# A three-group encoder layer in split fp32: another order of the last down products, and norms on VectorE

## The chip, the cores and the metric

The kernel runs on one core of one Trainium2 chip. The metric is the device time of one execution in microseconds; of the kernel before, three executions were timed, and one more was run under the hardware profiler.

## The reference

One layer of an encoder with post-norm and residual factor `ALPHA`, for a prompt of 512 tokens and a sample of 1024 tokens, width 1024, feed-forward width 4096, all in fp32:

```python
x = layer_norm(x, ln_in_g, ln_in_b)
x = layer_norm(ALPHA * x + token_mixer(x, w_in, rpb, g_mix_a, g_mix_b, w_out), ln1_g, ln1_b)
x = layer_norm(ALPHA * x + memory_cross_attention(x, mem, w_xq, w_xkv, w_xo), ln2_g, ln2_b)
x = layer_norm(ALPHA * x + squared_relu_mlp(x, w_up, w_down), ln3_g, ln3_b)
...
def squared_relu_mlp(x, w_up, w_down):
    return jnp.square(jax.nn.relu(x @ w_up)) @ w_down
```

`token_mixer` is dilated and neighbourhood attention, each half of its result under an rms norm, times `w_out`. `memory_cross_attention` has 4 heads over 256 memory tokens.

## The kernel before

The tokens form three groups of 512: group 0 is the prompt, 1 and 2 are the sample; a group has four tiles of 128 tokens. PE multiplies fp32r numbers, so each fp32 operand is split into a high part (a copy on ACT) and a low part (a subtraction on DVE or POOL), and each product is three matmuls: high x high, high x low, low x high.

The program runs in stages: memory keys and values, the mixers, the output projections (`y_tile`, `w_out_half` for groups 0 and 1, `w_out_part` for group 2), `ln1`, then `heads(gi, extra)` for the cross-attention of each group, then the MLP of group 0 (32 blocks up and down), and the MLP of the sample by seven products of a Strassen-like scheme, first UP, then DOWN. The order of instructions on each engine is set by the scheduler of the tile framework, which goes by the program's order, priorities and its own timing; tiles come from pools with a fixed number of buffers (tags such as tok 8, qt, pt, gb, kv 2 each, q 7, cpr 2, wh and wl 3, wraw 2), and a new tile waits for an old one's last reader.

`heads` takes a table `extra`: under the key (head, half) stand functions that are called in the midst of that head, so that one group's projections and norms lie beside another group's attention. In `heads(1, ...)` (L887 on) the four parts of group 2's output projection and its four norms `ln1(2, t)` are placed so. A `w_out_part` is accumulated into the tok tiles by DVE (L725). `layer_norm` (L148) takes its statistics on DVE (L154 to L157), raises the variance to -1/2 on POOL (`pow`, L158), subtracts the mean and multiplies by g on DVE (L162); then, with `spread=1`, ACT scales by 1/sigma (L169) and POOL adds b (L173); with `spread=0` a second DVE operation (L164) does both; with `spread=2` the first half takes L164's form at L167 and the second half has ACT scale and DVE add (L171). `split_t` transposes the normed tile on PE (L137), copies the high part out (L139) and subtracts for the low part on DVE (L140); the results are x10, x11, x12 by group, and y1 for the projections' input.

A DOWN product i has a left side of hidden blocks (one, or a sum or difference of two), a right side of blocks of `w_down`, and goes with a sign into one or two of four output blocks `accs`. It has 16 chunks; a chunk is 4 token tiles x 3 matmuls into 4 PSUM banks. `left_parts` (L1079) makes the left sum on DVE in a wraw tile (L1085), copies the high part on ACT (L1088) and subtracts on DVE (L1089). `right` loads a block to a q tile and a second one added onto it by a DMA of POOL's queue (L993), or subtracts two on DVE (L1003), and splits with L1008 (ACT) and L1009 (DVE). `collect` (L1099) empties a bank into `accs` on DVE (L1103, L1105). The last product, number 2, does the first three banks over 16 chunks and keeps the split right sides in `kept` tiles; meanwhile group 0 of the sample is finished (`finish`, a `layer_norm` with the statistics of L1072); then bank 4 takes 48 matmuls, for which the left side is made a second time, 128 columns at a time; then comes group 1's last tile.

```python
UP, DOWN = (5, 3, 2, 4, 1, 7, 6), (3, 5, 4, 7, 1, 6, 2)
1: (((0, 0), SUB, (1, 1)), ((0, 0), SUB, (1, 1)), (((0, 0), ADD), ((1, 1), ADD))),
2: (((1, 0), SUB, (1, 1)), ((0, 0),), (((1, 0), ADD), ((1, 1), SUB))),
6: (((1, 0), SUB, (0, 0)), ((0, 0), ADD, (0, 1)), (((1, 1), ADD),)),
```

## Time and profile before

| what | value |
|---|---|
| runs | 2379.4, 2380.44, 2386.65 us; median 2380.44 |
| profiled execution | 2383.99 us, of which 2382.2 is the span of its instructions |
| mean granted clock of PE | 0.990 |
| DOWN, from its first matmul to its last | 2042.88 to 2372.67 |
| heads(1), the part with group 2's projection and norms | about 1155 to 1248 |
| first norms ln1(0) | about 880 to 905 |

A row of the profile names the line, the engine, the operation and the tiles written and read. A wait is idle time of an engine just before an instruction, put down to what released it. The granted clock is a share of full speed (2.4 GHz); 0.5 is the lower of two levels (1.2 GHz), and a value in between is a mean over both.

### The profile page before, as it was taken

Reading aid. Unit: us, or ns where it says so; the run is one execution under the profiler, and the core shown is the slowest. Engines: PE = TensorE matmul, PEld = TensorE weight load, DVE = VectorE, ACT = ScalarE, POOL = GpSimd, SP = SyncE. Lnnn points to the kernel's source line nnn. Section 1 sums busy time; section 2 is a strip of 40 time slices with the busy share of each in tenths; the row PEclk is TensorE's granted clock in tenths of the full one; section 3 lists DMA queues with packets and bytes.
Section 4 is the critical chain, followed back from the end, with each engine's and each line's share of the span. In section 5 each row is a group of like instructions: output and inputs, shape, how many; then the busy total and the mean of one; then the engine's idle time right before and its main releaser. Section 6 shows DMA issues by size and latency. Waiting matters only on the chain. (4 is left out here: it accounts for less than half of the span.)

```text
span 2382.2 us, 33165 instructions
## 1 busy us (share of the span) xinstructions
PE 2293.0 (96%) x11128; PEld 1903.7 (80%) x11128; DVE 1614.3 (68%) x3305; ACT 1044.8 (44%) x2216; POOL 930.9 (39%) x836
## 2 busy tenths in 40 slices
PE   7999999999999999999989999999999999999987
PEld 6877788899888777878867877788888888888865
DVE  5256545777657776558566586777766686686987
ACT  4346655666555534333333333333354222344443
POOL 7555443222334125433154355555541324213152
PEclk9999999999999999999999999999999999999998
DMA  9676345544445543435325454444589999859762
GB/s 322 197 195 183 91 108 135 123 109 112 108 114 130 170 133 106 142 110 182 107 89 177 124 159 142 141 134 136 162 231 200 204 250 232 208 139 196 196 163 71
DMA packets 401530, 371.02 MB, mean 156 GB/s; under 512 B 72000, under 2 KB 317776, under 8 KB 401360
## 3 DMA queue, kind: packets, MB, share of 16 engines
q1 hardware_dynamic: 358352, 335.34, 47.8%
q0 software_dynamic: 43008, 33.56, 10.0%
q8 instruction: 88, 1.44, 0.3%
q14 instruction: 82, 0.67, 0.1%
HBM read 290.76 MB, written 52.98 MB: 144 GB/s over the span
## 5 line engine op out<-in xcount | busy, mean ns | idle before, releaser
L107 POOL TENSOR_TENSOR wl<-wraw,wh 128x512 fp32r<-128x512 f32 x80 | 106.0, 1340 | 173.9 <-ACT wh L106 158.5
L465 ACT ACTIVATE q<-q,st 128x256 f32<-128x256 f32 (+3 forms) x256 | 138.6, 546 | 70.7 <-DVE st L464 64.7
L1008 ACT ACTIVATE wh<-q 128x512 fp32r<-128x512 f32 x176 | 110.0, 626 | 134.6 <-DMA q<-in_w_up_dram 73.0
L1009 DVE TENSOR_TENSOR wh<-q,wh 128x512 fp32r<-128x512 f32 x176 | 126.1, 718 | 54.8 <-ACT wh L1008 54.5
L993 POOL DMA_DIRECT2D q<-in_w_up_dram x64 | 82.9, 1470 | 182.1 <-DVE h L1046 73.6
L312 POOL TENSOR_TENSOR wl<-wraw,wh 128x256 fp32r<-128x256 f32 x128 | 94.7, 763 | 143.3 <-ACT wh L311 122.2
L511 DVE TENSOR_TENSOR pt<-t,pt 128x512 fp32r<-128x512 f32 x160 | 105.4, 671 | 60.0 <-ACT pt L510 59.0
L946 POOL TENSOR_TENSOR wl<-pt,wh 128x512 fp32r<-128x512 f32 x64 | 91.5, 1450 | 118.9 <-ACT wh L945 118.8
L993 POOL DMA_DIRECT2D q<-in_w_down_dram x64 | 56.4, 976 | 199.5 <-DVE wraw L1085 66.1
L510 ACT ACTIVATE pt<-t 128x512 fp32r<-128x512 f32 x160 | 89.4, 583 | 75.3 <-PE o L523 72.4
L107 POOL TENSOR_TENSOR wl<-qt,wh 128x512 fp32r<-128x512 f32 x64 | 101.7, 1609 | 50.8 <-ACT wh L106 42.8
L523 PE MATMUL o<-pt,tok 128*128 128x256 f32 (+3 forms) x560 | 111.1, 312 | 4.0 <-ACT q L529 2.6
L119 POOL TENSOR_TENSOR wl<-wraw,wh 128x512 fp32r<-128x512 f32 x48 | 62.3, 1311 | 134.3 <-ACT wh L118 134.3
L959 DVE TENSOR_TENSOR tok<-tok,t 128x512 f32<-128x512 f32 x124 | 82.9, 680 | 37.0 <-PE t L131 37.0
L959 DVE TENSOR_TENSOR tok<-tok,s 128x512 f32<-128x512 f32 x124 | 83.9, 680 | 29.6 <-PE s L131 29.4
L131 PE MATMUL pj<-x20h,wl 128*128 128x512 f32 x256 | 101.2, 395 | 2.7 <-POOL wl L107 2.4
L129 PE MATMUL pj<-x20h,wh 128*128 128x512 f32 x256 | 100.6, 393 | 0.3 <-ACT wh L106 0.2
L130 PE MATMUL pj<-x20l,wh 128*128 128x512 f32 x256 | 100.0, 391 | 0.0
L507 PE MATMUL t<-ident,q 128*128 128x128 f32 x624 | 95.2, 273 | 5.0 <-ACT q L465 3.6
L1088 ACT ACTIVATE wh<-wraw 128x512 fp32r<-128x512 f32 (+2 forms) x96 | 53.0, 557 | 106.9 <-issue 42.3
L106 ACT ACTIVATE wh<-wraw 128x512 fp32r<-128x512 f32 x80 | 47.7, 626 | 103.5 <-PE pj L131 24.8
L945 ACT ACTIVATE wh<-pt 128x512 fp32r<-128x512 f32 x64 | 36.9, 624 | 122.0 <-PE s L131 103.0
(494 smaller groups left out, 7677.4 us busy)
## 6 DMA issues: line engine op xcount, KB each, us to landing
q<-in_w_up_dram SPq DMA_DIRECT2D x128, 256.0 KB
q<-in_w_down_dram SPq DMA_DIRECT2D x128, 256.0 KB
wraw<-in_w_in_dram SPq DMA_DIRECT2D x96, 256.0 KB
qt<-in_w_up_dram SPq DMA_DIRECT2D x32, 512.0 KB
pt<-in_w_down_dram SPq DMA_DIRECT2D x32, 512.0 KB
q<-in_w_up_dram POOLq DMA_DIRECT2D x64, 256.0 KB, 8.1
q<-in_w_down_dram POOLq DMA_DIRECT2D x64, 256.0 KB, 6.2
sa<-kv SPq DMA_DIRECT2D x28, 512.0 KB
```

The costliest lines, as they stand in the source:

```text
L107: G.tensor_sub(wl[:, sl], r, f32(wh[:, sl]))
L129: T.matmul(out, lh[k], rh[k], start=(k == 0), stop=False, skip_group_check=True)
L130: T.matmul(out, lh[k], rl[k], start=False, stop=False, skip_group_check=True)
L131: T.matmul(out, ll[k], rh[k], start=False, stop=(k == n - 1), skip_group_check=True)
L465: A.activation(p, p, AF.Exp, bias=nm, scale=scale, accum_out=den)
L507: T.transpose(t[:, x:x + P], p, ident)
L511: V.tensor_sub(lo[:, 0:x], t[:, 0:x], f32(hi[:, 0:x]))
L523: T.matmul(o[:, q0:q0 + n], v(c, h), part[:, x:x + n], start=(done == 0 and part is hi), stop=(done == total - 1 and part is lo), skip_gro ...
L959: V.tensor_add(x, x, q)
L993: G.dma_start(out, src, accum_op=ADD)
L1008: A.activation(dst[0], x, AF.Copy)
L1009: low.tensor_sub(dst[1], x, f32(dst[0]))
```

## The change

- `ln1` calls `layer_norm` with `spread=0`, for all three groups.
- `heads(1)`: two of group 2's `w_out_part` calls stand at (1, 1) and the last at (2, 0); the norms stand at (2, 1) and (3, 0). The tile Y[2] is made ahead of `heads(0)`.
- DOWN's order is 4, 7, 1, 5, 3, 6, 2. The squares of block (1, 1) are taken in UP's last product, those of (0, 0) in DOWN's first.
- The left sums of products 2 and 6 are made in place, in the hidden blocks (1, 1) and (0, 0), by `left_sum` (L1081 after the change).
- Group 0 of the sample is finished in product 6 with `spread=0`; g3 lies in cpr tiles and b3 in q tiles, loaded after product 3.
- In the last product the left high parts of all chunks stay in tok tiles and the low parts of the last 128 columns in a qt and a pt tile, so that bank 4 uses parts made before. The four tiles of group 1 are collected and finished after it.

Lines behind L884 have other numbers after the change: L1009 is L1010, L1003 is L1004, L1085 is L1081, L1089 is L1093 (and L1095 for 128 columns), L1105 is L1111, L1072 is L1073.

```diff
--- before.py
+++ after.py
@@ -726,7 +726,7 @@
 
     def y_tile(gi, t):
         r, row = req(gi), 0 if gi < 2 else 512
-        if t == 0:
+        if gi not in Y:
             Y[gi] = new_act(f"y{gi}")
         rows = slice(row + t * P, row + (t + 1) * P)
         if toks[gi][t] is None:
@@ -774,7 +774,7 @@
         if t == 0:
             X1[gi] = new_act(f"x1{gi}")
             GB[gi] = [[bcast(d[n][0], "gb")] for n in ("ln1_g", "ln1_b")]
-        layer_norm(toks[gi][t], *GB[gi], 1)
+        layer_norm(toks[gi][t], *GB[gi])
         split_t(toks[gi][t], *X1[gi], t * P)
 
     def qt(gi, h, c):
@@ -881,11 +881,12 @@
         ln1(0, i)
         if i < 2:
             w_out_half(1, i)
+    Y[2] = new_act("y2")
     heads(0, {(h, 0): [call(ln1, 1, h)] for h in range(4)} | {(h, 1): [call(y_tile, 2, h)] for h in range(4)})
     heads(1, {(0, 0): [call(ln2, 0, 0), call(ln2, 0, 1)], (0, 1): [call(ln2, 0, 2), call(ln2, 0, 3)],
-              (1, 0): [call(w_out_part, 2, 0)], (1, 1): [call(w_out_part, 2, 1)],
-              (2, 0): [call(w_out_part, 2, 2)], (2, 1): [call(w_out_part, 2, 3)],
-              (3, 0): [call(ln1, 2, 0), call(ln1, 2, 1)], (3, 1): [call(ln1, 2, 2), call(ln1, 2, 3)]})
+              (1, 0): [call(w_out_part, 2, 0)], (1, 1): [call(w_out_part, 2, 1), call(w_out_part, 2, 2)],
+              (2, 0): [call(w_out_part, 2, 3)], (2, 1): [call(ln1, 2, 0), call(ln1, 2, 1)],
+              (3, 0): [call(ln1, 2, 2), call(ln1, 2, 3)]})
     heads(2, {(h, 0): [call(ln2, 1, h)] for h in range(4)})
     w_xo_part(2, 3)
     for t in range(4):
@@ -905,7 +906,7 @@
         6: (((1, 0), SUB, (0, 0)), ((0, 0), ADD, (0, 1)), (((1, 1), ADD),)),
         7: (((0, 1), SUB, (1, 1)), ((1, 0), ADD, (1, 1)), (((0, 0), ADD),)),
     }
-    UP, DOWN = (5, 3, 2, 4, 1, 7, 6), (3, 5, 4, 7, 1, 6, 2)
+    UP, DOWN = (5, 3, 2, 4, 1, 7, 6), (4, 7, 1, 5, 3, 6, 2)
 
 
     def left(i, k):
@@ -1044,7 +1045,7 @@
                     A.activation(h, o, AF.Copy, scale=1.0 if op == ADD else -1.0)
                 else:
                     V.tensor_tensor(h, h, o, op=op)
-            b = {2: (0, 1), 7: (1, 0), 6: (0, 0)}.get(i)
+            b = {2: (0, 1), 7: (1, 0), 6: (1, 1)}.get(i)
             if b is not None:
                 square(b, f)
 
@@ -1076,18 +1077,23 @@
         row = 512 * h + t * P
         S.dma_start(outs[1][0, row:row + P], accs[h][t])
 
-    def left_parts(lw, c, t0, t1):
-
-        n = (t1 - t0) * P
-        x = hidden(lw[0], c)[:, t0 * P:t1 * P]
-        if len(lw) > 1:
-            y = wp.tile([P, 512], F32, name="wraw", tag="wraw", bufs=2)[:, 0:n]
-            V.tensor_tensor(y, x, hidden(lw[2], c)[:, t0 * P:t1 * P], op=lw[1])
-            x = y
+    def left_sum(lw, c, y):
+        V.tensor_tensor(y, hidden(lw[0], c), hidden(lw[2], c), op=lw[1])
+
+    def left_parts(lw, c, summed=None, hi=None, last=None):
+
+        x = hidden(summed or lw[0], c)
+        if len(lw) > 1 and summed is None:
+            x = wp.tile([P, 512], F32, name="wraw", tag="wraw", bufs=2)
+            left_sum(lw, c, x)
         a = wp.tile([P, 1024], F32R, name="wh", tag="wh")
-        A.activation(a[:, 0:n], x, AF.Copy)
-        V.tensor_sub(a[:, 512:512 + n], x, f32(a[:, 0:n]))
-        return [(a[:, j * P:(j + 1) * P], a[:, 512 + j * P:512 + (j + 1) * P]) for j in range(t1 - t0)]
+        hi, lo = a[:, 0:512] if hi is None else hi, a[:, 512:1024]
+        n = 512 if last is None else 384
+        A.activation(hi, x, AF.Copy)
+        V.tensor_sub(lo[:, 0:n], x[:, 0:n], f32(hi[:, 0:n]))
+        if last is not None:
+            V.tensor_sub(last, x[:, n:512], f32(hi[:, n:512]))
+        return [(hi[:, j * P:(j + 1) * P], last if j * P == n else lo[:, j * P:(j + 1) * P]) for j in range(4)]
 
     def chunk(banks, ls, rs, c):
         for o, (lh, ll) in zip(banks, ls):
@@ -1104,43 +1110,53 @@
             else:
                 V.tensor_tensor(x, x, o, op=op)
 
+
+    inplace = {2: (1, 1), 6: (0, 0)}
+    g3 = b3 = None
     for n, i in enumerate(DOWN[:-1]):
         lw, rw, into = PRODUCTS[i]
         banks = [bank(tag) for tag in (("pj", "pj", "s", "s") if n % 2 == 0 else ("t", "t", "t", "o"))]
         for c in range(16):
-            ls = left_parts(lw, c, 0, 4)
+            ls = left_parts(lw, c, inplace.get(i))
             chunk(banks, ls, right(rw, down_block(c), V, "wl"), c)
             if n == 0:
-                square((1, 1), c)
+                square((0, 0), c)
+            if i == (5, 3)[c % 2]:
+                left_sum(PRODUCTS[2][0], c, hidden(inplace[2], c))
+            if i == 3:
+                left_sum(PRODUCTS[6][0], c, hidden(inplace[6], c))
+            if i == 6 and c % 4 == 2:
+                finish(0, c // 4, 0)
         for t in range(4):
             collect(into, t, banks[t])
-        if i in (5, 1):
+        if i in (5, 3):
             for t in range(4):
-                stats(0, t, 1 if i == 5 else 0)
+                stats(0, t, int(i == 3))
+        if i == 3:
+            g3, b3 = [slot("cpr") for _ in range(2)], [slot("q", 512) for _ in range(2)]
+            for q, name in ((g3, "ln3_g"), (b3, "ln3_b")):
+                for j in range(2):
+                    src = d[name][0]
+                    S.dma_start(q[j], bass.AP(tensor=src.tensor, offset=src.offset + 512 * j, ap=[[0, P], [1, 512]]))
 
 
     lw, rw, into = PRODUCTS[DOWN[-1]]
-    g3, b3 = ([slot("q", 512) for _ in range(2)] for _ in range(2))
-    for q, name in ((g3, "ln3_g"), (b3, "ln3_b")):
-        for j in range(2):
-            src = d[name][0]
-            S.dma_start(q[j], bass.AP(tensor=src.tensor, offset=src.offset + 512 * j, ap=[[0, P], [1, 512]]))
-    kept = []
+    kept, ls, rs = [], [], []
     banks = [bank(tag) for tag in ("pj", "pj", "s", "s")]
     for c in range(16):
         if c % 8 == 0:
             kept.append([act.tile([P, 8, 512], F32R, name="kept", tag="act") for _ in range(2)])
-        rs = right(rw, down_block(c), V, dst=[k[:, c % 8] for k in kept[c // 8]])
-        chunk(banks[0:3], left_parts(lw, c, 0, 3), rs, c)
-        if c % 4 == 3:
-            finish(0, c // 4, 1)
-    for t in range(3):
+            kept_lo = slot("qt" if c == 0 else "pt", dt=F32R)
+        if c % 2 == 0:
+            kept_hi = slot("tok", dt=F32R)
+        rs.append(right(rw, down_block(c), V, dst=[k[:, c % 8] for k in kept[c // 8]]))
+        ls.append(left_parts(lw, c, (1, 1), kept_hi[:, c % 2 * 512:c % 2 * 512 + 512],
+                             kept_lo[:, c % 8 * P:c % 8 * P + P]))
+        chunk(banks[0:3], ls[c][0:3], rs[c], c)
+    for c in range(16):
+        chunk(banks[3:4], ls[c][3:4], rs[c], c)
+    for t in range(4):
         collect(into, t, banks[t])
-    for c in range(16):
-        chunk(banks[3:4], left_parts(lw, c, 3, 4), [k[:, c % 8] for k in kept[c // 8]], c)
-    for t in range(4):
-        if t == 3:
-            collect(into, 3, banks[3])
         finish(1, t, 2 if t == 3 else 1)
```

The scheduler moves instructions at places that the diff does not tell. On DVE in heads(1), from the first norm of group 2 on, the order before was (tok holds the projection, lnst the statistics, gb gains and offsets, cpr the attention's probabilities):

```order
L162 SCALAR_TENSOR_TENSOR tok<-tok,lnst,gb 128x1024
L725 TENSOR_TENSOR tok<-tok,o 128x512
L810 RECIPROCAL cst<-cst 128x2
L156 BN_AGGR lnst<-lnst 128x2
L725 TENSOR_TENSOR tok<-tok,pj 128x512
L812 TENSOR_SCALAR cpr<-cpr,cst 128x256 x2
L157 TENSOR_SCALAR lnst<-lnst 128x1
L162 SCALAR_TENSOR_TENSOR tok<-tok,lnst,gb 128x1024
L725 TENSOR_TENSOR tok<-tok,pj 128x512
```

and is now:

```order
L162 SCALAR_TENSOR_TENSOR tok<-tok,lnst,gb 128x1024
L725 TENSOR_TENSOR tok<-tok,o 128x512
L156 BN_AGGR lnst<-lnst 128x2
L725 TENSOR_TENSOR tok<-tok,pj 128x512
L164 SCALAR_TENSOR_TENSOR tok<-tok,lnst,gb 128x1024
L157 TENSOR_SCALAR lnst<-lnst 128x1
L162 SCALAR_TENSOR_TENSOR tok<-tok,lnst,gb 128x1024
L725 TENSOR_TENSOR tok<-tok,pj 128x512
L154 BN_STATS lnst<-tok 128x6
L155 BN_STATS lnst<-tok 128x6
L832 TENSOR_TENSOR q<-o,q 128x512
```

The probabilities' L810 and L812 are gone from this stretch, and a second pass of the norm, L164, stands in front of the next tile's.

On DVE in product 1 of DOWN the order before was, for a chunk and the start of the next (h are hidden blocks, wraw the left sum, wh the split parts, cpr the right difference):

```order
L1085 TENSOR_TENSOR wraw<-h_17051,h_17374 128x512
L1003 TENSOR_TENSOR cpr<-q 128x512
L1089 TENSOR_TENSOR wh<-wraw,wh 128x512
L1009 TENSOR_TENSOR wh<-cpr,wh 128x512
L1085 TENSOR_TENSOR wraw<-h_17052,h_17375 128x512
L1089 TENSOR_TENSOR wh<-wraw,wh 128x512
```

and is now (h_17362 is block (1, 1), tok is block (1, 0)):

```order
L1010 TENSOR_TENSOR wh<-cpr,wh 128x512
L1081 TENSOR_TENSOR wraw<-h_17039,h_17362 128x512
L1004 TENSOR_TENSOR cpr<-q 128x512
L1081 TENSOR_TENSOR h_17362<-tok,h_17362 128x512
L1093 TENSOR_TENSOR wh<-wraw,wh 128x512
L1010 TENSOR_TENSOR wh<-cpr,wh 128x512
L1111 TENSOR_TENSOR qt<-qt,t 128x512 x2
L1081 TENSOR_TENSOR wraw<-h_17039,h_17362 128x512
L1111 TENSOR_TENSOR pt<-pt,t 128x512
```

The sums in place for product 2, which the program calls in products 5 and 3, are issued here, 16 of them up to product 1's end.

On DVE in product 6 of DOWN (its finish in qt and pt, g in q tiles before and in cpr now) the order before was, where the finish began in product 6:

```order
L1085 TENSOR_TENSOR wraw<-tok,h_17052 128x512
L162 SCALAR_TENSOR_TENSOR qt<-qt,st,q 128x512 x2
L162 SCALAR_TENSOR_TENSOR pt<-pt,st,q 128x512 x2
L1089 TENSOR_TENSOR wh<-wraw,wh 128x512
L1009 TENSOR_TENSOR wh<-q,wh 128x512
L162 SCALAR_TENSOR_TENSOR qt<-qt,st,q 128x512 x2
L162 SCALAR_TENSOR_TENSOR pt<-pt,st,q 128x512 x2
```

and is now:

```order
L162 SCALAR_TENSOR_TENSOR pt<-pt,st,cpr 128x512 x2
L157 TENSOR_SCALAR st<-st 128x1
L162 SCALAR_TENSOR_TENSOR pt<-pt,st,cpr 128x512 x2
L1093 TENSOR_TENSOR wh<-h_17039,wh 128x512
L1010 TENSOR_TENSOR wh<-q,wh 128x512
L164 SCALAR_TENSOR_TENSOR qt<-qt,st,q 128x512 x3
L1093 TENSOR_TENSOR wh<-h_17039,wh 128x512
L164 SCALAR_TENSOR_TENSOR qt<-qt,st,q 128x512
L1010 TENSOR_TENSOR wh<-q,wh 128x512
L164 SCALAR_TENSOR_TENSOR pt<-pt,st,q 128x512 x3
L1093 TENSOR_TENSOR wh<-h_17040,wh 128x512
```

Both passes of all four tiles now stand in this one stretch, which ends at chunk 8.

## Rows read from the trace of the kernel before

**Rows 1.** The page, busy time of each engine and its share of the span.

```profile
PE 2293.0 (96%) x11128; PEld 1903.7 (80%) x11128; DVE 1614.3 (68%) x3305; ACT 1044.8 (44%) x2216; POOL 930.9 (39%) x836
```

**Rows 2.** Waits of PE, 870 to 940: line, what ended them; total, times, longest.

```profile
PE t L137 <- DVE y1l L140: 3.3, 1, 3.3
```

**Rows 3.** PE in short windows: length, PE busy (matmuls), granted clock, DMA share, GB/s.

```profile
900.00:904.00 4.00, 4.00 (x13) 0.60 0.25 89
1214.00:1218.00 4.00, 4.00 (x16) 0.60 0.00 0
1231.00:1238.00 7.00, 6.40 (x20) 0.52 0.40 106
2294.00:2304.00 10.00, 8.18 (x36) 1.00 0.25 81
2354.00:2368.00 14.00, 9.93 (x21) 0.52 0.19 75
```

**Rows 4.** Waits of PE in heads(1), 1155 to 1248.

```profile
PE t L137 <- POOL tok L173: 4.5, 2, 3.1
PE pj L129 <- DVE tok L725: 3.6, 1, 3.6
PE o L129 <- ACT pt L822: 0.8, 1, 0.8
```

**Rows 5.** One window, all engines: PE, PEld, DVE, ACT, POOL busy, granted clock.

```profile
1210.00:1225.00 15.00, 9.85 (x44) 7.82 (x44) 14.36 (x22) 6.83 (x11) 11.48 (x7) 0.89 0.18 54
```

**Rows 6.** PE in the last three products of the down projection, by windows.

```profile
2217.14:2260.66 43.52, 43.52 (x194) 1.00 0.73 202
2260.66:2307.24 46.58, 44.47 (x194) 1.00 0.63 139
2307.24:2372.67 65.43, 52.85 (x193) 0.84 0.33 113
```

**Rows 7.** Waits of PE in the down projection, 2042 to 2383.

```profile
PE s L1096 <- DVE wh L1089: 5.4, 4, 2.4
PE pj L1094 <- ACT wh L1088: 4.6, 1, 4.6
PE t L1095 <- DVE wh L1009: 2.0, 2, 1.8
```

**Rows 8.** Timeline of DVE beside ln1(0): start, length, line, operation.

```profile
893.96 3.04 DVE L162 SCALAR_TENSOR_TENSOR tok<-tok,lnst,gb 128x1024 f32<-128x1024 f32 x1
...
896.99 1.27 DVE L162 SCALAR_TENSOR_TENSOR tok<-tok,lnst,gb 128x1024 f32<-128x1024 f32 x1
```

**Rows 9.** Timeline of POOL beside ln1(0).

```profile
891.18 4.74 POOL L173 TENSOR_TENSOR tok<-tok,gb 128x1024 f32<-128x1024 f32 x2
```

**Rows 10.** Groups of POOL in heads(1), 1155 to 1248: busy us, mean ns.

```profile
L119 POOL TENSOR_TENSOR wl<-wraw,wh 128x512 fp32r<-128x512 f32 x12 | 15.3, 1289 | 54.4 <-ACT wh L118 54.4
...
L107 POOL TENSOR_TENSOR wl<-wraw,wh 128x512 fp32r<-128x512 f32 x6 | 8.7, 1469 | 8.8 <-ACT wh L106 5.3 <-issue 3.5
```

**Rows 11.** Timeline of DVE in the sixth product.

```profile
2293.86 1.41 DVE L162 SCALAR_TENSOR_TENSOR pt<-pt,st,q 128x512 f32<-128x512 f32 x2
2295.18 0.68 DVE L1085 TENSOR_TENSOR wraw<-tok,h 128x512 f32<-128x512 f32 x1
2295.79 0.68 DVE L1089 TENSOR_TENSOR wh<-wraw,wh 128x512 fp32r<-128x512 f32 x1
```

**Rows 12.** Groups of POOL in the down projection, 2042 to 2383.

```profile
L158 POOL TENSOR_TENSOR st<-st,mhalf 128x1 f32<-128x1 f32 x4 | 8.1, 2038 | 0.0
...
L173 POOL TENSOR_TENSOR gb<-gb,q 128x512 f32<-128x512 f32 x4 | 6.4, 1619 | 0.0
L158 POOL TENSOR_TENSOR lnst<-lnst,mhalf 128x1 f32<-128x1 f32 x4 | 3.6, 892 | 48.7 <-DVE lnst L157 48.7
```

**Rows 13.** The page, DMA issues: KB each, median us to landing.

```profile
q<-in_w_down_dram POOLq DMA_DIRECT2D x64, 256.0 KB, 6.2
```

**Rows 14.** Timeline of DVE, its last operation.

```profile
2377.78 0.69 DVE L171 TENSOR_TENSOR kv<-kv,q 128x512 f32<-128x512 f32 x1 [0.18 <-ACT kv L169]
```


## The prediction, made blind

> **What bounds the kernel.** I read the page first. TensorE (PE) is busy 96% of the span and DVE 68% [rows 1], so a change can only win where PE stands still or where its clock was lowered. Next I asked for PE's waits by stretch; the reader is to see that they lie in few places, and that DVE or something in DVE's queue ends almost all of them. Last I read PE's granted clock in short windows at those places, for a second price: there it stands near half in the rows, so PE does its work at 1.2 instead of 2.4 GHz for some microseconds.
>
> Three places touch the change.
>
> A, the first norms of group 0 beside `w_out_half(1, ·)`: one wait of 3.3 on a y1l that DVE issues late [rows 2]. Over 900 to 904 the clock is 0.60 [rows 3], which costs 4 x 0.40 = 1.6. Lost: 4.9.
>
> B, heads(1), where group 2 gets its output projection and norms: waits of 4.5 on POOL's L173, 3.6 on DVE's L725 and 0.8 on ACT [rows 4]. DVE is busy 14.36 of the 15 us from 1210 [rows 5]. The clock is 0.60 for 4 us and 0.52 for 7: 1.6 + 3.4 = 5.0 [rows 3]. Lost: 13.9.
>
> C, the down projection. A product without a wait takes 43.52; the sixth takes 46.58 and the last 65.43 [rows 6], so 3.1 + 21.9 = 25.0 are lost. The waits name the culprits: the low parts of the left side for bank 4 (5.4), one piece that stood behind a late load (4.6), a right part behind DVE (2.0) [rows 7]. The clock stands at 0.52 from 2354 to 2368 [rows 3], and that belongs to the 25.0.
>
> **The change, part by part.**
>
> *Norms of ln1 on DVE.* Each of 12 tiles gives up one ACT pass and one POOL addition and gets a second DVE pass of the L162 kind. Alone such a pass takes 1.27; beside POOL's L173 (two in 4.74) it took 3.04 [rows 8, 9]. So a tile trades 2.37 on POOL, and the stretching, for 1.27 on DVE.
>
> At A, DVE ran before its y1l two L162 passes, 3.04 + 1.27 with 0.2 of small work. Now it runs two second passes, 2.5, and the other two L162 come behind. y1l is about 2.0 sooner, and a wait of about 1.3 is left. The 1.6 of clock should then go too: gain 3.6, taken as 3.5. Bounds: 0, if DVE turns out as late from other work, and 4.9.
>
> At B, all norm work now stands in DVE's queue: 8 passes x 1.27 = 10.2, of which 4 are new, 5.1. They lie half a head sooner, beside three projection parts in a row, so the transposes of the normed tiles no longer wait for POOL (4.5 gone). What is late next is an L725 that empties a pj bank and stands behind an L162 and two L140: 1.27 + 2 x 0.61 = 2.5, of which PE can't cover some 2. POOL still runs weight splits there, L107 at 1.47 mean [rows 10]; two of them that hold a DVE pass cost up to 2.9. I take 2 + 3 = 5 lost in place of 13.9: gain 9. Bounds: 5, if the clock's 5.0 stays lost with half the waits, and 13.
>
> The Trainium skill (SBUF — State Buffer, Who interferes with whom) has a rule that speaks against this placement: a DVE instruction with two SBUF inputs and a GpSimd one that reads SBUF exclude each other, whichever starts first. The 3.04 of [rows 8] agrees. By that rule alone, if each of the 8 passes met one split, the price would be 8 x 1.47 = 11.8 and B would give nothing; the total would then be about 2365. I do not take it, since all splits (L119 and L107) keep POOL busy for 15.3 + 8.7 = 24 of the stretch's 93 us [rows 10], so that about a quarter of the passes meets one.
>
> The new loads on SP (w_out sooner, ln1's gains and the xq weights later) all have more than one chunk of PE work ahead of them, so I cost them at nothing; uncovered, one would cost PE a wait like the 4.6 of [rows 7].
>
> *Order 4, 7, 1, 5, 3, 6, 2 with left sums in place.* The sums of products 2 and 6 are made once, in place, instead of as 32 temporaries (plus 16 for bank 4). But the built order issues the 16 sums into (1,1) during product 1. There DVE then has 5 operations for a chunk: the temporary, the low parts of both sides, the right's difference, the sum in place. From the collects ahead of the product to chunk 15, I count 71 operations in the order. They start 0.61 apart [rows 11]: 43.3, against 15 chunks x 2.72 = 40.8 on PE. Stall 2.5, less a small lead, taken as 2 (0.3 to 4). The starts of products 7, 5 and 3 wait for a right part behind eight collects: 0.8 together (0 to 3).
>
> *Group 0's finish in product 6, on DVE.* The order bunches it: between the collects and chunk 8's low part DVE has 8 collects, 14 low parts, 4 statistics (26 x 0.61 = 15.9), 0.8 of aggregates and 16 norm passes x 0.66 [rows 11] = 10.6. Sum 27.3, against 8 x 2.72 + 0.9 = 22.7 on PE: 4.6 short, in two or three pieces. DVE's second passes stand behind a `pow` on POOL, four of which took 8.1 [rows 12]; I add 1.4 for that. Stall 6 (3 to 12). What is queued behind: low parts of the left and right side of chunks 6 to 8, for which PE waits. I add no lower clock, since the wait of 2.0 in product 6 left it at 1.00 [rows 3, 7]. The loads keep five of seven q slots, 5 x 2.72 = 13.6 ahead, against an accumulating transfer of 6.2 [rows 13] with some 4 of load and split: covered, unless POOL's queue grows.
>
> *Last product.* Bank 4's 48 matmuls find both sides split already, since the left high parts lie in tok slots and the low columns in qt and pt. DVE and ACT have nothing to do for them; their 11 us run through, and the stall of the last product, 21.9, goes to 0.
>
> *Tail.* Before, three tiles of group 1 were normed while bank 4 crept. Now that stretch lasts 37 matmuls from the end of the other banks, 8.4 us, and the norms do not fit. From there DVE needs about 6.5 (ten operations) to the first `pow`, then POOL is in line: `pow` 0.9, four L173 halves at 1.62, `pow`, two halves more (2.6), the last tile's `pow` [rows 12], and some 2 of closing passes; with overlap 18.5, so 10.1 past the last matmul against 5.8 now (2372.67 to 2378.47) [rows 6, 14]. Loss 4.3 (2 to 7).
>
> C in sum: 25.0 - 2 - 0.8 - 6 - 4.3 = 11.9, taken as 12. The bounds, with all parts at one end, are 1.5 and 18.5.
>
> **The sum.** 3.5 + 9 + 12 = 24.5 against the profiled run's 2383.99 (span 2382.2): 2359.5. That run lies 3.55 above the median of the runs, 2380.44; from the median it is **2356**. Everything else of PE's order is unchanged, and I cost it at nothing.
>
> **Rivals.**
>
> 1. *DVE remains the pacer in heads(1).* For it: 14.36 of 15 us busy, and the change gives DVE 5.1 more. The clock's 5.0 stay lost, and B gives 2 and A 2: total 16, **2364**. Against: the longest passes were long only beside L173, which is gone.
>
> 2. *POOL's queue in product 6.* DVE waits for a `pow` in one piece: 8.1, what four took together, with an accumulating load queued behind it. One window then runs at 0.52 for 14 us, 6.7 lost. Beyond the 1.4 that I have, that is 13.4 more: total 11, **2369**. Against: three of the four can only have been short, as the mean is 2.04 with a first one that waited.
>
> 3. *The clock, and slower.* The stalls in products 1 and 6 are small, but many. In 2354 to 2368 a chain of small waits kept the clock at 0.52 [rows 3]; each such stretch costs 6.7. Two eat C's gain. Four of them, in products 1 (once), 6 (twice) and at a product's start, take 26.8; with A and B at 2 each, the total is 2 + 2 + 12 - 26.8 = -10.8: **2391**. It decides from the third stretch on. Against: at half clock a chunk takes 5.4, DVE gains 2.4 on PE in each, so a stretch should end itself; and the 2.0 above.
>
> 4. *The waits only change places in the down projection.* C gives 0 to 2, since the stalls are what DVE lacks in time, wherever it lacks it; with A and B as forecast: total 13, **2367**. Against: 21.9 of the 25.0 lie in the last product alone, and the change takes DVE's work out of its last stretch.
>
> **Chances.** Forecast 0.62 (2344 to 2374 if all its bounds fall on one side, most of it 2349 to 2364), rival 1 0.13, rival 2 0.09, rival 3 0.06, rival 4 0.10. A range of 2343 to 2371 leaves out rival 3 and the ends of the rest. About 0.3%, 7 us, is what a measurement of this kernel tells from no change: under 2373 is faster. Faster 0.83, same 0.10 (the upper ends of rivals 2 and 4, mixtures of 1 and 2), slower 0.07.
>
> **What would show it.** Right: no wait over 1.5 us near the former places A and B, the clock 1.00 there; the last product 43.5 long, its last 48 matmuls without a wait; waits on low parts in chunks 5 to 9 of product 6, about 6 in sum, and about 2 in the second half of product 1, on L1010 or L1093; a tail of about 10 past the last matmul. Wrong: a clock window near 0.5 in products 1 or 6, a `pow` over 3 us with DVE idle behind it, DVE passes of 3 us beside L107 in heads(1), or a tail over 13.

## The result, and the profile after

The changed kernel takes 2362.78 us at the median of four runs (2356.73 to 2366.54), against 2382.12 for the kernel before, measured four times beside it: a ratio of 0.9915, 95% interval 0.9887 to 0.9942. That is 19.3 us less. The forecast was 2356, 24.4 below the median it started from; the measured time lies within the range.

The profiled execution of the changed kernel has a span of 2359.8, 22.4 less than before. PE's share on the page, which answers to [rows 1]:

```profile
PE 2286.3 (97%) x11128; PEld 1902.1 (81%) x11128; DVE 1607.9 (68%) x3309; ACT 1024.8 (43%) x2180; POOL 881.2 (37%) x816
```

PE is busy 7 us less in sum, since less of its work is done at the lower clock, and the rest of the 22.4 is idle time that went.

**Beside ln1(0).** The waits of PE from 870 to 955 (in total, times, longest), to be read against [rows 2]:

```profile
PE s L129 <- ACT qt L788: 2.4, 1, 2.4
...
PE t L137 <- DVE y1l L140: 1.0, 1, 1.0
```

The wait on y1l is 1.0 instead of 3.3, and no stretch of lower clock follows it. But a wait of 2.4 has come in its place, at the first scores of heads(0), behind ACT's L788, and behind that wait PE works for 3.4 us at the lower clock, 0.50. The window of PE there (length, busy, granted clock, DMA share, GB/s), and ACT's timeline, which shows why PE waited:

```profile
946.70:950.10 3.40, 3.40 (x13) 0.50 0.36 106
```

```profile
944.95 0.63 ACT L106 ACTIVATE wh<-wraw 128x512 fp32r<-128x512 f32 x1 [3.52 <-DMA wraw<-in_w_xq_dram]
```

ACT stood 3.52 us at a copy of a w_xq block that had not landed, with L788 behind it in its queue. SP's timeline names the loads' start (issue start, length, count), in the kernel before and then in the changed one:

```profile
922.61 17.44 SPq L92 DMA_DIRECT2D wraw<-in_w_xq_dram  x8
```

```profile
925.68 23.09 SPq L92 DMA_DIRECT2D wraw<-in_w_xq_dram  x10
```

**In heads(1).** PE's waits from 1155 to 1280, against [rows 4]:

```profile
PE pj L129 <- DVE tok L725: 2.5, 2, 1.6
```

The POOL waits are gone, and two on L725, of 1.56 and 0.96, are left.

**The stages by time.** Windows of PE in the changed kernel (length, PE busy with its matmuls, granted clock, DMA share, GB/s): first a stretch of 418 matmuls around ln1(0) and the start of heads(0), from the one that a wait on L771 precedes, then 600 matmuls of heads(1), then products 1 and 6 and the last product of DOWN, and what follows the last matmul:

```profile
883.13:972.22 89.09, 85.61 (x418) 0.98 0.36 113
1154.86:1279.89 125.03, 122.03 (x602) 1.00 0.44 140
...
2116.07:2164.05 47.98, 45.71 (x193) 1.00 0.53 169
...
2251.80:2299.71 47.91, 44.95 (x193) 1.00 0.86 206
2299.71:2344.73 45.02, 44.39 (x193) 1.00 0.15 50
2344.73:2359.78 15.05, 0.00 (x0) 0.66 0.35 140
```

The same matmuls in the kernel before:

```profile
881.22:971.59 90.37, 86.00 (x418) 0.98 0.36 110
1155.57:1292.65 137.08, 126.95 (x602) 0.96 0.40 128
...
2372.67:2382.22 9.55, 0.00 (x0) 0.77 0.14 56
```

So the first stretch gained 1.3 (90.37 to 89.09), heads(1) 12.05 (137.08 to 125.03), the last product 20.4 (65.43 in [rows 6], 45.02 now). Product 1 lost 4.5 against 43.52, product 6 takes 47.91 where the sixth product took 46.58 before, and the tail grew by 5.5 (9.55 to 15.05). The seven products and the tail together fell by 8.5: before, 329.79 from the first matmul to the last and 9.55; now 315.75 and 15.05.

Whole runs of one kernel spread by 10 us here (2356.73 to 2366.54), and stretches that no edit touches end up to 10 us apart: the same matmul, ahead of all changes, came at 758.29 in the profile of order_417 and at 768.82 in that of place_back. Up to there PE's clock stood at 0.5 for 3.4 us in the first and for 17 us in the second, which makes some 7 of the 10; where the rest comes from was not followed up. The experiments are therefore read by stages.

### The profile page after: what moved, and what is told of

Same layout as the page of the kernel before. It is cut to its first block, busy times and chain, and to the rows that moved or that the text cites. A ratio compares the mean times of both kernels' runs of the same rounds, so it can differ in the third digit from the quotient of the medians.

```text
span 2359.8 us, 33087 instructions
## 1 busy us (share of the span) xinstructions
PE 2286.3 (97%) x11128; PEld 1902.1 (81%) x11128; DVE 1607.9 (68%) x3309; ACT 1024.8 (43%) x2180; POOL 881.2 (37%) x816
## 3 DMA queue, kind: packets, MB, share of 16 engines
q0 software_dynamic: 43008, 33.56, 10.1%
q8 instruction: 88, 1.44, 0.3%
## 5 line engine op out<-in xcount | busy, mean ns | idle before, releaser
L107 POOL TENSOR_TENSOR wl<-wraw,wh 128x512 fp32r<-128x512 f32 x80 | 107.5, 1357 | 204.3 <-ACT wh L106 158.5
L1009 ACT ACTIVATE wh<-q 128x512 fp32r<-128x512 f32 x176 | 110.1, 626 | 139.6 <-DMA q<-in_w_up_dram 79.3
L1010 DVE TENSOR_TENSOR wh<-q,wh 128x512 fp32r<-128x512 f32 x176 | 125.8, 716 | 56.2 <-ACT wh L1009 52.9
L107 POOL TENSOR_TENSOR wl<-qt,wh 128x512 fp32r<-128x512 f32 x64 | 101.6, 1608 | 50.6 <-ACT wh L106 42.5
L119 POOL TENSOR_TENSOR wl<-wraw,wh 128x512 fp32r<-128x512 f32 x48 | 66.6, 1404 | 106.5 <-ACT wh L118 100.0
L158 POOL TENSOR_TENSOR lnst<-lnst,mhalf 128x1 f32<-128x1 f32 x44 | 51.1, 1162 | 103.3 <-DVE lnst L157 103.3
```

Source lines behind the costliest of these rows:

```text
L107: G.tensor_sub(wl[:, sl], r, f32(wh[:, sl]))
L1009: A.activation(dst[0], x, AF.Copy)
L1010: low.tensor_sub(dst[1], x, f32(dst[0]))
```

## The experiments

**norms_back** puts the norms back on ACT and POOL and leaves the rest.

```diff
-        layer_norm(toks[gi][t], *GB[gi])
+        layer_norm(toks[gi][t], *GB[gi], 1)
```

> The changed kernel with the ln1 norms back on ACT and POOL (scale on ACT, addition of b on POOL), for all three groups; the new places in heads(1) and the new down projection stay. Theory: the second DVE pass is what shortens both places. Then the wait on the late y1l beside ln1(0) returns, about 3.3 us with the clock at half for some 3 us (4 to 5 us lost there), the wait of 2.4 us at the first scores of heads(0) goes away (it came from weight loads that started 3 us later behind the DVE passes), and in heads(1) transposes wait for POOL's L173 again, 3 to 6 us lost. In sum 5 to 8 us slower than the changed kernel. Rival: the new places alone do it and the engine of the norms does not matter: within 2 us of the changed kernel in both stretches.

Measured: 2362.15 (ratio to the kernel before 0.991, 0.9895 to 0.9925), no different from the changed kernel. The stretch around ln1(0) and heads(1), in windows of PE:

```profile
882.20:972.82 90.62, 86.90 (x419) 0.96 0.35 108
1158.06:1282.20 124.14, 122.09 (x601) 1.00 0.44 139
```

and the waits of PE from 870 to 955:

```profile
PE t L137 <- DVE y1l L140: 3.4, 1, 3.4
```

Around ln1(0) the theory holds in kind: the y1l wait is 3.4 again, the clock falls with it, and the wait on L788 is gone. But the stretch takes 90.62, only 1.5 more than with the norms on DVE, which is within the 2 us of the rival. In heads(1) the theory falls: 124.14 is 0.9 less than with the norms on DVE. Once the norms lie half a head sooner, POOL's additions are early enough, and it does not matter who does them. So by size the rival holds in both stretches.

**place_back** is the other half: norms on DVE, the calls at their old places.

```diff
-              (1, 0): [call(w_out_part, 2, 0)], (1, 1): [call(w_out_part, 2, 1), call(w_out_part, 2, 2)],
-              (2, 0): [call(w_out_part, 2, 3)], (2, 1): [call(ln1, 2, 0), call(ln1, 2, 1)],
-              (3, 0): [call(ln1, 2, 2), call(ln1, 2, 3)]})
+              (1, 0): [call(w_out_part, 2, 0)], (1, 1): [call(w_out_part, 2, 1)],
+              (2, 0): [call(w_out_part, 2, 2)], (2, 1): [call(w_out_part, 2, 3)],
+              (3, 0): [call(ln1, 2, 0), call(ln1, 2, 1)], (3, 1): [call(ln1, 2, 2), call(ln1, 2, 3)]})
```

> The changed kernel with group 2's projection parts and norms back at their old places in heads(1); the norms stay on DVE and the down projection new. Theory: at the old places the four norms meet the last projection part and DVE is full there, so 4 to 8 of the 10.8 us that heads(1) gained are lost again, with one wait over 2 us on an L725 behind the norm passes and the clock at half once or twice. Rival: the norms on DVE alone did it, since all POOL waits are gone; then under 3 us are lost in heads(1).

Measured: 2370.73 (0.9944, 0.9928 to 0.9961). Its 600 matmuls of heads(1), and PE's longest wait there:

```profile
1159.03:1291.65 132.62, 125.98 (x601) 0.97 0.41 132
```

```profile
PE t L137 <- DVE lnst L157: 2.2, 1, 2.2
```

132.62: 7.6 of the 12.05 are lost (the expectation wrote 10.8 for that gain), within the 4 to 8 expected, with a wait over 2 us and the clock down once. The wait is not on L725, as the theory had it: it is on a transpose, which starts right after a norm's second pass (L164, from 1226.95 to 1228.80). With norms_back this gives the full square: 137.08 with neither, 132.62 with the norms on DVE, 124.14 with the places, 125.03 with both. The places are worth 12.9 by themselves, the norms 4.5 without them and nothing with them.

**heads_only** has both of these and the down projection of before (the edits of `ln1`, `heads` and `Y[2]` in the diff ahead, nothing else).

> The kernel before with the changed norms and the changed places in heads(1) alone; the down projection as before. Theory: the gains add up and nothing downstream gives back: the down projection starts about 14 us sooner and its last product still takes about 65 us and the sixth about 46.6; time about 2368, 13 to 16 us under the kernel before. Rival: the two halves depend on each other (loads or buffers of the down projection are disturbed by the earlier end), and the down projection changes by over 3 us.

Measured: 2372.27 (0.9955, 0.9939 to 0.9972), 10.9 under the kernel before in the same runs, less than the 13 to 16 expected. The down projection is untouched: its sixth product takes 46.45 (46.58 before), and the last, by its window, 65.89 (65.43 before), with the clock as low as before:

```profile
2294.99:2360.88 65.89, 53.56 (x193) 0.84 0.32 112
```

The halves are independent; the first is worth about 11 to 12 and the second the remaining 8 to 9.

**order_417** swaps products 7 and 1.

```diff
-    UP, DOWN = (5, 3, 2, 4, 1, 7, 6), (4, 7, 1, 5, 3, 6, 2)
+    UP, DOWN = (5, 3, 2, 4, 1, 7, 6), (4, 1, 7, 5, 3, 6, 2)
```

> The changed kernel with the down products in the order 4, 1, 7, 5, 3, 6, 2. The 16 sums in place into block (1, 1) then fall beside product 7, whose right side is added by DMA, so DVE has 4 operations a chunk (2.41 us at 0.602) instead of 5 (3.01) against 2.72 on PE. Theory: product 1 took 47.98 because DVE paced it, 16 x 5 x 0.602 = 48.2; here both products take 43.5 to 44, and the whole is 4 to 4.5 us faster than the changed kernel. Rival: the sums only move the stall (DVE short of time in product 7 behind eight collects, or its accumulating loads late on POOL): gain under 1.5 us.

First, why product 1 is slow in the changed kernel. Its window for DVE (length, DVE busy with its operations, the clock of PE, DMA share, GB/s):

```profile
2116.07:2164.05 47.98, 47.98 (x80) 1.00 0.53 169
```

DVE has no pause in the whole product: 80 operations, 0.60 us from one to the next. With the new order, products 1 and 7 by windows:

```profile
2070.80:2114.82 44.02, 43.84 (x194) 1.00 0.66 191
2114.82:2158.86 44.04, 43.82 (x194) 1.00 0.77 180
```

44.02 + 44.04 against 43.52 + 47.98: 3.4 us less. The theory holds, a little under its size, since each of the two now loses half a microsecond at its start. In whole runs it is 2358.31 (0.9896, 0.9881 to 0.9911), whose interval overlaps that of the changed kernel.

**last_remade** makes bank 4's left side a second time, as before the change.

```diff
     for c in range(16):
-        chunk(banks[3:4], ls[c][3:4], rs[c], c)
+        a = wp.tile([P, 1024], F32R, name="wh", tag="wh")
+        x = hidden((1, 1), c)[:, 384:512]
+        A.activation(a[:, 0:P], x, AF.Copy)
+        V.tensor_sub(a[:, 512:512 + P], x, f32(a[:, 0:P]))
+        chunk(banks[3:4], [(a[:, 0:P], a[:, 512:512 + P])], rs[c], c)
```

> The changed kernel, but bank 4 of the last product gets its left side made again, 128 columns a chunk on ACT and DVE, as before the change; all else stays, so the sums are in place and group 0's finish is out of the way. Theory: remaking the parts beside the first norms of group 1, in DVE's queue, was what made the last product long, together with the clock that falls there; the last product takes 53 to 60 us instead of 45.0, and what follows its last matmul is 4 to 5 us shorter than the 15.05 now. Rival: the late load and group 0's norms in the last product did it; then bank 4 runs through and the product stays under 48.

Measured (one run): 2369.04. Windows of the last product and the tail, and PE's waits there:

```profile
2302.95:2357.67 54.72, 46.86 (x193) 1.00 0.18 60
2357.67:2367.23 9.56, 0.00 (x0) 0.74 0.27 110
```

```profile
PE s L1102 <- DVE wh L1160: 4.7, 4, 1.8
```

54.72, as expected, with 4.7 of waiting on the parts made again (L1160), and the tail falls back to 9.56. Together 64.3 against 60.1 of the changed kernel: keeping the parts saves 9.7 in the product and gives 5.5 of it back, because bank 4's slow matmuls were also the time in which DVE normed three tiles. The clock did not fall in this run: PE was busy for 46.86 at a clock of 1.00, where the kernel before had 52.85 at 0.84 [rows 6]. So of the other 10.7 of the old 65.43, 6.0 are longer busy time and 4.7 idle time. The late load of [rows 7] and group 0's finish both left the last product with the change; which of them lowered the clock, and what each is worth, was not tried apart.

**finish_pool** puts group 0's finish in product 6 on ACT and POOL.

```diff
-                finish(0, c // 4, 0)
+                finish(0, c // 4, 1)
```

> The changed kernel with group 0's finish in product 6 back on ACT and POOL (scale on ACT, addition of b on POOL). Theory: product 6 took 47.91 since DVE is short of 4.4 us; with 8 of its 16 norm passes gone (5.3) it would have enough, but the 8 additions on POOL (1.3 to 1.6 each) hold up DVE's operations that read two tiles from SBUF, so that part of it is lost again: product 6 at 44 to 46. Rival: the hold-up costs more than the passes save, product 6 at 48 or above, with DVE operations of 1.6 us and more beside POOL, as in the kernel before.

Measured (one run): 2372.88. Product 6 by its window; two lines of DVE's timeline in it, and POOL's beside the second; then the second in the changed kernel:

```profile
2254.15:2309.64 55.49, 47.12 (x193) 0.94 0.77 181
```

```profile
2273.12 3.02 DVE L1093 TENSOR_TENSOR wh<-h,wh 128x512 fp32r<-128x512 f32 x1 [0.46 <-ACT wh L1092]
...
2281.64 6.30 DVE L1095 TENSOR_TENSOR qt<-h,tok 128x128 fp32r<-128x128 f32 x8
```

```profile
2281.12 4.33 POOL L173 TENSOR_TENSOR pt<-pt,q 128x512 f32<-128x512 f32 x3
...
2286.04 1.55 POOL L173 TENSOR_TENSOR pt<-pt,q 128x512 f32<-128x512 f32 x1
```

```profile
2279.14 1.70 DVE L1095 TENSOR_TENSOR qt<-h,tok 128x128 fp32r<-128x128 f32 x8
```

The rival holds, and by more than it asked: 55.49, 7.6 longer. Eight small subtractions that take 1.70 in the changed kernel take 6.30 beside four POOL additions, and a full one 3.02 instead of 0.68. DVE saves 5.3 of passes and loses more to POOL. Not all of the 7.6 is DVE's: PE waited up to 4.4 at once, and the clock fell (0.94 over the product), which costs some 3 of it. The finish on DVE was the right choice. The kernel before had the same loss at the start of its last product: from 2302.91 on, four DVE operations of 384 and 512 columns take 1.63 to 1.79 each beside L173.

**tail_dve** gives the second tile of group 1 to DVE.

```diff
-        finish(1, t, 2 if t == 3 else 1)
+        finish(1, t, (1, 0, 1, 2)[t])
```

> The changed kernel with the second tile of group 1 finished on DVE alone, so that POOL has two additions less ahead of the last tile's pow. Theory: the tail is set by POOL's queue (four additions in 5.09 us, then pow, ACT, additions, pow): the time from the last matmul to the end falls from 15.05 by 1.3 to 2.2 us. Rival: DVE is as full as POOL there, and its two passes more (1.35) cost what POOL saves: within 0.5 us.

Measured (one run): 2366.52; the tail by its window:

```profile
2348.30:2364.75 16.45, 0.00 (x0) 0.62 0.32 128
```

16.45: 1.4 longer, so the rival's reason holds, and the loss is over the 0.5 that it allowed. In the changed kernel's tail DVE works almost without a pause to the last tile. Four lines of its timeline there:

```profile
2335.37 2.48 DVE L1111 TENSOR_TENSOR gb<-gb,pj 128x512 f32<-128x512 f32 x4 [4.66 <-PE pj L1102]
...
2350.68 2.41 DVE L162 SCALAR_TENSOR_TENSOR kv<-kv,lnst,cpr 128x512 f32<-128x512 f32 x2
2353.53 1.75 DVE L167 SCALAR_TENSOR_TENSOR kv<-kv,lnst,q 128x512 f32<-128x512 f32 x1 [0.44 <-POOL lnst L158]
2355.20 0.68 DVE L171 TENSOR_TENSOR kv<-kv,q 128x512 f32<-128x512 f32 x1
```

From 2335.37, when three banks end together, to 2355.88 are 20.5 us, with only one pause of 0.44. So DVE waited for POOL only that 0.44, and tail_dve shows that more work on DVE costs time. But POOL is in it too. Three stretches of DVE's work take longer beside POOL's additions than alone: twice 2.4 for two passes of L162 (1.41 alone), and 1.75 for L167 (0.75 in last_remade). That is 3.0 of the 20.5. The chain of work that ended last also runs through POOL's queue from 2343.26 on. Both engines are full in the tail, and what it takes without the stretching was not tried.

**fin_gate** spreads group 0's finish.

```diff
-            if i == 6 and c % 4 == 2:
-                finish(0, c // 4, 0)
+            if i == 6 and c == 11:
+                late = [slot("q", 512) for _ in range(2)]
...
+            if i == 6 and c in (2, 6, 11, 12):
+                finish(0, (2, 6, 11, 12).index(c), 0, late if c >= 11 else None)
```

> The changed kernel with group 0's finish spread over product 6: b3 lies in the two wraw tiles, and the third and fourth tile take a second copy of g3 that is loaded behind chunk 10's blocks, so that they cannot be finished earlier; the same operations on the same engines. Theory: the stall in product 6 is a burst, not a lack of DVE time over the product (its operations sum to about 38 us): 47.91 falls to 44 to 45, total 3 to 4 us less. Rival: what paces product 6 is the wait for pow or loads on POOL's queue; then it stays over 46.5.

Measured (one run): 2363.09. Product 6, the last product and the tail:

```profile
2250.37:2296.61 46.24, 44.86 (x194) 1.00 0.86 220
2296.61:2340.40 43.79, 43.79 (x193) 1.00 0.11 38
2340.40:2361.32 20.92, 0.00 (x0) 0.61 0.25 101
```

Product 6 falls to 46.24, less than hoped; the last product runs without a wait. But the tail is 20.92. The end is not set by PE: DVE's collection of the first three banks began 85.2 after product 6's start (2335.60), and in the changed kernel 83.6 after it (2335.37 - 2251.80). PE had the same work, but the built order put more of bank 4's matmuls ahead of the other banks' last ones. Behind the last matmul of the first two banks 20 matmuls were left, against 40 in the changed kernel. So what product 6 saved went into bank 4's matmuls, and the three banks, from whose end the tail is counted, ended no sooner. At 46.24 neither side of the expectation came: the theory had 44 to 45, the rival over 46.5.

**two_two** ends two banks first, then the others.

```diff
-        chunk(banks[0:3], ls[c][0:3], rs[c], c)
-    for c in range(16):
-        chunk(banks[3:4], ls[c][3:4], rs[c], c)
+        chunk(banks[0:2], ls[c][0:2], rs[c], c)
+    for t in (2, 3):
+        for c in range(16):
+            chunk(banks[t:t + 1], ls[c][t:t + 1], rs[c], c)
```

(with room for the low parts of 256 columns in two qt and two pt tiles).

> The changed kernel, with the last product in another shape: banks 0 and 1 over all chunks first, then bank 2 alone, then bank 3 alone, from kept parts (the low parts of 256 columns a chunk lie in two qt and two pt tiles). Theory: the time behind the last matmul, 15.05, is DVE's work on four tiles that starts when three banks end together (20.5 us of DVE from there); if the first two tiles end 22 us ahead of the last matmul and the third 11 us ahead, only the last tile is left and the tail is 9.5 to 10.5, as in the kernel before, with the last product still at 44 to 46: total 4 to 5.5 us less. Rival: the first half, with a chunk every 1.36 us, is paced by the right side's loads and splits, and PE waits there for as much as the tail gains.

Measured (one run): 2361.43; the tail by its window, and the start of DVE's collection:

```profile
2347.16:2359.63 12.47, 0.00 (x0) 0.64 0.42 168
```

```profile
2334.82 2.48 DVE L1111 TENSOR_TENSOR gb<-gb,pj 128x512 f32<-128x512 f32 x4 [4.83 <-PE pj L1102]
```

Half of it: the tail is 12.47, 2.6 less, and the last product 45.36. The two tiles end 12.3 us ahead of the last matmul, not 22, since the scheduler put bank 2's matmuls among the first half's.

**best417** is two_two with order_417.

> The kernel of the run before this one in this list, with the order 4, 1, 7, 5, 3, 6, 2. Theory: the two gains lie in different stretches and add: 8 to 9 us under the changed kernel, about 2354. Rival: they meet in DVE's or the loads' lead before the last products, and the sum is under 5 us.

Measured: 2360.25 in five runs (0.9896, 0.988 to 0.9911), the same as order_417 alone in whole runs. Its last product and tail:

```profile
2297.41:2343.90 46.49, 44.82 (x193) 1.00 0.15 51
2343.90:2356.38 12.48, 0.00 (x0) 0.61 0.42 168
```

58.97 against 60.22 of order_417 (45.16 and 15.06): by stages the gains add to 4.5 (3.4 in products 1 and 7, 1.1 here against the changed kernel's 60.07) instead of the hoped 8 to 9, under the 5 that the rival named, and whole runs can't tell that from order_417.

**best_gate** adds the spread finish.

> The same with group 0's finish spread over product 6 (third and fourth tile behind a second copy of g3 that is loaded late, b3 in the wraw tiles). Theory: with the tail no longer set by when three banks end, the 1.7 us that the spreading took from product 6 (46.24 instead of 47.91) now reach the end: 1 to 3 us under the other. Rival: the copy's loads delay the right sides of the last product, and nothing is gained.

Measured: 2360.68 (0.9903, 0.9886 to 0.9919). Product 6 and the tail:

```profile
2250.06:2299.86 49.80, 45.74 (x193) 0.97 0.82 220
...
2343.77:2361.14 17.37, 0.00 (x1) 0.60 0.30 121
```

The rival holds: nothing is gained. Product 6's stretch has one wait of 4.0, on the high part of a right side of the last product, and the tail is 17.37; that the copy's loads caused the wait was not tried alone.

**best_strict** forces the order that two_two meant, by PSUM buffers.

```diff
+        if t > 1:
+            banks[t] = bank("pj")
+            for c in range(16):
+                chunk(banks[t:t + 1], ls[c][t:t + 1], rs[c], c)
```

> The order 4, 1, 7, 5, 3, 6, 2 and the last product in the shape of two_two, but banks 2 and 3 take the PSUM buffers of banks 0 and 1, so that their matmuls can't be put among the first half's. In two_two they were, and the first two tiles ended only 12 us ahead of the last matmul instead of 22; the tail was 12.47. Theory: now the first two tiles end about 21 us ahead, the third 11, and the tail is 9.5 to 10; the last product takes 44 to 47 with one wait of about 1 us where bank 2 needs its buffer: 3 to 6 us under the kernel with the order alone. Rival: the first half is paced by loads and splits, a chunk every 1.36 us on PE, and PE waits there for 3 us or more, with no gain.

Measured: 2364.16 (0.992, 0.9902 to 0.9939). The last product, the tail, and PE's waits:

```profile
2301.70:2352.49 50.79, 45.10 (x193) 1.00 0.22 78
2352.49:2362.06 9.57, 0.00 (x0) 0.75 0.14 55
```

```profile
PE pj L1102 <- DVE wh L1093: 4.5, 3, 3.0
...
PE pj L1100 <- DVE gb L1111: 1.2, 1, 1.2
```

The tail is 9.57, as in the kernel before, and the last product pays for it with 50.79: 4.5 of waiting on low parts at its start, up to 2310.63, where DVE also collects product 6 and splits the right sides, and 1.2 where bank 2 needs its buffer. The sum is 60.36, no gain. In all kernels here with the new down projection the sum of last product and tail stayed at 58 to 65, while the split between PE's waits and the tail changed. A likely reason is that DVE's work for the last tiles has to lie somewhere; that was not tried by taking work away.

## Why the prediction was right

**A, forecast 3.5, measured 1.3 (1.4 over all kernels).** The y1l step was right: it was to win 3.6, of which 2.0 were of the wait and 1.6 of the clock. The same matmul behind the y1l wait came at 901.32 instead of 903.29, and since the changed kernel had reached the wait on L771 1.9 later (883.13 against 881.22), that is 3.9 sooner by the stage; the wait left is 1.0, where 1.3 was forecast. The step that failed was the one that costed the new loads on SP at nothing. The w_xq loads started 3.1 later (925.68 against 922.61), and one uncovered copy cost PE 2.4 at the head of heads(0). The lower clock behind that wait (0.50 for 3.4 us) cost little: it came in five of the twelve kernels here with the norms on DVE, which take 89.2 for these 418 matmuls in the mean, against 89.0 in the seven without it. That the norms' engine causes it is shown by norms_back, where the wait is gone and y1l's is back; that the path runs through DVE's weight splits, which now stand behind the second passes and free the wraw tiles later, is read from the order and SP's timeline and was not tried alone. All twelve together take 89.1 (88.71 to 89.65), against 90.37 and 90.62 in the two with the norms on POOL, so the small gain is clear of the scatter.

**B, forecast 9, measured 12.05.** The size was close and inside the bounds (5 to 13), but part of the reason was wrong. The prediction gave the 4.5 of POOL's waits to the norms' move to DVE and to the new places together; norms_back shows that the places alone take them away. Of what is late next, one step held: L725 behind an L162 and two L140, 2 expected and 1.56 measured. The price of contention, taken as 3, was 0.96. That is the other wait on L725. DVE's timeline ahead of it, and the matmul that waited:

```profile
1185.54 2.03 DVE L164 SCALAR_TENSOR_TENSOR tok<-tok,lnst,gb 128x1024 f32<-128x1024 f32 x1
...
1187.56 2.25 DVE L162 SCALAR_TENSOR_TENSOR tok<-tok,lnst,gb 128x1024 f32<-128x1024 f32 x1
1189.73 0.67 DVE L725 TENSOR_TENSOR tok<-tok,pj 128x512 f32<-128x512 f32 x1
```

```profile
1190.46 0.50 PE L129 MATMUL pj<-wh,q 128*128 128x512 f32 x1 [0.96 <-DVE tok L725]
```

The two passes took 2.03 and 2.25 beside POOL's weight splits (L107, 1185.20 to 1188.72), against 1.27 alone. So L725 came 1.7 later, and PE waited 0.96; at 1.27 each the wait should not have been there, which is worked out from these rows and was not tried. The passes of all eight norms in heads(1) took 1.66 (L164) and 1.44 (L162) in the mean; behind the others PE had other work. The rule of the Trainium skill (SBUF — State Buffer, Who interferes with whom) agrees with these stretched passes, but the forecast by it alone, that B would give nothing, did not come: most of its price was paid by DVE, not by PE. Both waits that are left are shorter than forecast, and the clock stayed at 1.00; that is 2.5 of the 3 more that B gave.

**C, forecast 12, measured 8.5.** Term by term:

- The last product's 21.9 go to 0: 1.5 was left (45.02 against 43.52). last_remade shows that 9.7 of it hung on the parts made twice.
- Product 1, taken as 2, was 4.5. The count of 71 operations was right: from the first collect at 2117.72 to the end of chunk 15's low part at 2160.54 they take 42.82, where 43.3 was forecast. The mis-sized step is the lead. The prediction took some off the 2.5 for a lead of DVE; but the collects began 1.65 after PE's first matmul of the product, and PE had 3.51 of work behind the last low part and not one chunk of 2.72, since DVE makes the low parts of two chunks close together: 1.65 + 42.82 + 3.51 = 47.98, as measured. order_417 confirms that DVE's operations set the pace, by taking one a chunk away.
- The starts of products 7, 5 and 3, 0.8: 0.0, 0.2 and 0.5.
- Product 6, taken as 6, was 4.4: 3.0 in three waits of 0.8 to 0.95 and one of 0.35, and 1.4 as longer busy time of PE (44.95). DVE's shortage of 4.6 was the right term; the 1.4 for `pow` was not needed, since the four took 6.2 together with DVE busy in between. finish_pool showed the alternative to be 7.6 worse.
- The tail, taken as 4.3 longer, was 5.5. The length from three banks' end was 20.5 and not 18.5. The terms of the working add to 20.3; the step that failed is the 1.8 taken off for overlap. DVE's passes did not run beside POOL's additions for nothing: they took 3.0 longer there. To DVE's last operation, as the prediction counts it, the tail is 11.15 (5.8 before), where 10.1 was forecast.

In sum 25.0 - 1.5 - 4.5 - 0.7 - 4.4 - 5.5 = 8.4, within its bounds (1.5 to 18.5). These bounds are added wrong: with all parts at one end they are -1.0 (25.0 - 4 - 3 - 12 - 7) and 19.7. The measured sum lies within either.

**The sum.** The parts were 3.5 + 9 + 12 = 24.5, and came as 1.3 + 12.05 + 8.5 = 21.9, with some 0.5 in stretches that were not forecast. A and C came 5.7 short and B 3.05 over, so that the total fits better than its parts; that is luck. Two of the prediction's signs of being right also failed: a wait of 2.4 and a clock of 0.50 stand near the former place A, and a wait of 1.56 in heads(1), where it had none over 1.5 and a clock of 1.00. Of its signs of being wrong none came (the tail by its own count, 11.15).

**The rivals.** Rival 1 did not come: the clock in heads(1) is 1.00. Rivals 2 and 3 neither: no wait of a microsecond in products 1 and 6 and a clock of 1.00 in every product. Rival 4 names what happened in part: 11.1 of the 25.0 came back as lost time of PE (4.5, 0.7, 4.4 and 1.5) and 5.5 in the tail, nearly all of it behind DVE, in the tail behind POOL as well. It stopped short of its price, 8.5 instead of 0 to 2. Part of the work that bank 4 waited for is no longer done at all, which last_remade puts at 4.2 of product and tail together (64.3 against 60.1); the rest is not split further.

## What to carry to other kernels

Count an engine's operations for each chunk against the chunk's time on the engine that should set the pace, since an excess of 0.3 us a chunk (3.01 against 2.72 here) adds up over the product, and count from when the engine can begin. Read in the built order where an added operation falls, and order the products so that it falls beside one with time to spare. Where a slow last part also covers the next step's work, count both together: what the part gains, the tail gives back in part.

## What was not expected of the hardware

Eight subtractions of 128 x 128 took 6.30 us beside POOL additions and 1.70 without. The four that met an addition took 1.38 to 1.58 each, about as long as the additions there (1.33 to 1.74); the other four took 0.28, as all eight do in the changed kernel. So in this trace the price of meeting POOL goes by the length of POOL's operation and not by the size of DVE's, and many small DVE operations pay it many times. And waits of 0.8 to 0.95 in a row, 3.9 us apart, left the clock at 1.00 in product 6.
